# FFN modulation groups of 2, 4, 6 and 4 k-tiles in a transformer block on one Trainium2 core

## The chip, the core and the metric

One core of a Trainium2 chip runs the whole program. TensorE (PE in the views) does the matmuls and transposes, with its weight loads shown apart (PEld); VectorE (DVE), ScalarE (ACT) and GpSimd (POOL) do the elementwise work; SyncE's queue (SP) issues nearly all transfers. The metric is the time of one execution on the device in microseconds, the median of several.

## The reference

The program computes one transformer block for 256 tokens of width 2048 in float32. The part that matters here is the second half, the feed-forward network with its adaptive modulation:

```python
mod = jax.nn.silu(c) @ w_ada[l] + b_ada[l]
shift_m, scale_m, gate_m, shift_f, scale_f, gate_f = jnp.split(mod, 6, axis=-1)
...
o = jnp.concatenate([o_n, o_m], axis=-1) @ w_o[l]
x = x + gate_m[:, None, :] * rms_norm(o, post_norm_mix[l])
h = modulate(rms_norm(x, pre_norm_ffn[l]), shift_f, scale_f)
f = jnp.square(jax.nn.relu(h @ w_up[l])) @ w_down[l]
x = x + gate_f[:, None, :] * rms_norm(f, post_norm_ffn[l])
```

`modulate` is `h * (1 + scale) + shift`. `w_up` is 2048 x 8192, so the contraction of the up-projection has 16 k-tiles of 128 rows. The modulation vector of each of these k-tiles needs its own 2 x 128 columns (shift and scale) of `w_ada`, over all 2048 rows.

## The kernel before

**Stages.** In order of time: input modulation and input projections, compressed and windowed attention, the second attention (`moba`) beside the first half of the output projection (`wo`), the second half of `wo`, `after_mixer`, the up-projection (`up`), the down-projection (`dps`, `dn`), the end.

**Matmuls in three products.** Weights arrive as float32 and are split in two parts: `split` (lines 539 to 545) casts a 128 x 1024 tile to fp32r on ScalarE (`hi`, L544) and subtracts it on VectorE (`lo`, L545). Each product is then three matmuls of 512 columns (`products`, lines 549 to 551): hi x hi, hi x lo and lo x hi. The split tiles have WBUFS = 5 buffers of either kind; a "spare" split goes to the pool `acc` (16 buffers) instead, which holds the 16 results `facc` of the up-projection too, and `oacc` and `xm`.

**Units and the stream.** The work of these stages is a list of units. A unit may have a load (a transfer into one of RAWBUFS = 5 raw buffers of 1 MB), a prep (the splits, or steps of a gemv) and a main (the matmuls). `Stream.run` emits loads as far ahead as raw buffers allow, preps up to AHEAD = 4 units ahead while the splits they hold stay within 5, and mains in order. The framework's scheduler then orders each engine's queue by this priority and by what is ready; `tc.high_priority()` moves work forward. Queues run in that fixed order on the chip.

**The up-projection** runs in four passes, one for each group of k-tiles in `F_GROUPS`. A pass goes over 8 blocks of 1024 output columns; a block has one unit per k-tile, and a load for each two of them. A unit makes 12 matmuls: 2 token tiles, 2 column halves, 3 products. Its sums are in PSUM banks of the pool `mm`, which has 5. At a block's end `up_done` evicts four banks: ScalarE copies them to `facc` in the first pass (L1160), VectorE adds them to `facc` in the others (L1162). The first eight units of the first pass are "token major": their main does token tile 0 of all eight and then token tile 1.

**The modulation groups.** Each group of `F_MODS` is a `mod_units`: a gemv over the 2048 rows of `w_ada`, 16 k-tiles of rows, on VectorE. The first step multiplies by a scalar (L318), the 15 others multiply and add into one tile in a chain (L323); a step's width is 256 columns per k-tile of the group. `krows` steps share a raw buffer: 4 for a group of 2 k-tiles, 2 for 4, 1 for 6. After the last step TensorE transposes the result (L377), VectorE sums it (L379), ScalarE modulates the k-tiles (L414) and casts them (L417), and VectorE subtracts (L418).

The first group's gemv runs beside `wo`, and `after_mixer` applies its modulation to the first k-tiles of each token tile as it transposes them (`x2t`, L1108); the other k-tiles are copied to `xnf` (L1115). Group i's gemv, for i of 1 to 3, is spread by `spread` over pass i - 1, from position `start` to position `at` of its units, and its last unit stands ahead of the remaining ones.

Of the kernel before, what the change touches and what calls it, by code (L numbers as in the profile page):

```python
# [48 lines left out]
M_PLAIN = 2  # L49

M_DIRECT = (3, 7, 11)
F_MODS = (4, 4, 4, 4)
F_GROUPS = ((0, 4), (4, 8), (8, 12), (12, 16))

F_FIRST = 1
F_AT = (0, 1, 2)
# [81 lines left out]
def spread(base, extra, first, last):  # L138

    out = list(base[:first])  # L140
    n = len(extra)
    at = [first + (i * (last - first)) // max(n, 1) for i in range(n)]
    i = 0
    for j in range(first, len(base) + 1):
        while i < n and at[i] <= j:
            out.extend(extra[i])
            i += 1
        if j < len(base):
            out.append(base[j])
    while i < n:  # L150
        out.extend(extra[i])
        i += 1
    return out
# [3 lines left out]
def tile_adaln_block(ctx: ExitStack, tc: tile.TileContext, x, c, w_ada, b_ada, g_pm, g_qm, w_in,  # L157
# [262 lines left out]
    def gate_units(tag, gpost, hold, whole=True):  # L420

        name = f"gate{tag}"
        acc = Acc(True)
        base = 2 * D if tag == "m" else 5 * D

        def first():
            acc.t = gp.tile([P, D], F32, tag="ga", name=name)
            nc.gpsimd.memset(acc.t, 0.0)
            nc.sync.dma_start(acc.t[0:1, :], b_ada[:, base:base + D])

        units = gemv_units(name, base, D, False, 1, acc, first)

        st = {}

        def load():
            st["raw"] = rawtile(f"{name}post")
            nc.sync.dma_start(st["raw"], gpost.partition_broadcast(P))

        def part(q):
            b = bank(f"{name}b{q}")  # L440
            qs = slice(q * 512, (q + 1) * 512)
            hi, lo = (pair(f"{name}{n}{q}", F32R).rearrange("p a b -> p (a b)") for n in ("hi", "lo"))
            split2(acc.t[:, qs], hi, lo)
            nc.tensor.matmul(b, onesr, hi, start=True, stop=False)
            nc.tensor.matmul(b, onesr, lo, start=False, stop=True)
            nc.vector.tensor_mul(acc.t[:, qs], b, st["raw"][:, qs])
            hold["G"] = acc.t

        def main():
            for q in range(4):  # L450
                part(q)

        hold["part"] = part
        if whole:
            units.append(Unit(load, None, main, free="main"))
        else:
            units.append(Unit(load))
        return [[u] for u in units]
# [59 lines left out]
    def token_major(us, between=None, parts=1):  # L518


        halves = [u.half for u in us]

        def main():
            for t in range(NT):
                if t and parts > 1:
                    for n in range(parts):
                        for h in halves:
                            h(t, (n,))
                else:
                    for h in halves:  # L530
                        h(t)
                if between is not None:
                    between(t)

        for u in us[:-1]:
            u.main, u.rel = None, 0
        us[-1].main, us[-1].rel = main, sum(u.w for u in us)
# [15 lines left out]
    def banks(name):  # L553
        ps = {}

        def of(ci, t, first):
            if first:
                ps[ci, t] = mbank(f"{name}_{ci}_{t}")
            return ps[ci, t]

        return of
# [411 lines left out]
    def call(f):  # L973
        return [Unit(None, None, f)]

    def in_units(name, k0, k1):

        c0, parts, dsts = blocks[name]
        return weight_units(f"in_{name}{k0}", w_in, list(range(k0, k1)), c0, parts, hs,
                            banks(f"in_{name}{k0}"), in_done(name, dsts, parts), plain=M_PLAIN)  # L980

    def flat(lists):
        return [u for b in lists for u in b]
# [15 lines left out]
    base = flat(in_units(n, 0, 2) for n in ("kv", "kw", "qn", "vm", "km")) + turn0[:2]  # L999
    stream.add(spread(base, mods[1], 1, len(base) - 1))  # L1000
    base = turn0[2:] + flat(in_units(n, 2, 6) for n in ("km", "vm", "qn", "kw")) + turn1[:4]
    base.insert(3, Unit(None, late_constants))
    stream.add(spread(base, mods[2], 0, len(base) - 3))
    base = turn1[4:] + flat(in_units(n, 6, 10) for n in ("kw", "qn", "vm", "km")) + turn2[:4]
    stream.add(spread(base, mods[3], 0, len(base) - 3))
    base = turn2[4:]
# [3 lines left out]
    base = per[0] + per[1] + call(cmp_inputs) + call(keys)  # L1010
# [45 lines left out]
    xnf, fstat = [], {}  # L1056
    k0s = np.cumsum((0,) + F_MODS).tolist()
    ffn_mods = [mod_units("f", k0, n, xnf, fstat) for k0, n in zip(k0s, F_MODS)]

# [6 lines left out]
    def keep_mod(k0, n, last):  # L1066
        def main():
            f = last.reduce()
            x2h["mod"].update((k, f(k)) for k in range(k0, k0 + n))
        return [Unit(None, None, main)]  # L1070

    first_mods = [g for k0, n, m in zip(k0s, F_MODS, ffn_mods[:F_FIRST])
                  for g in m[:-1] + [keep_mod(k0, n, m[-1][0])]]
# [6 lines left out]
    def after_mixer(t):  # L1080

        x2 = x2h["x"]
        n0 = F_GROUPS[0][1]
        if t == 0:
# [68 lines left out]
    def up_done(blk, g):  # L1153
        def done(ci, t, b):
            n = blk * 2 + ci
            if n not in facc:
                facc[n] = chunk(f"facc{n}")
            dst = facc[n][:, t, :]
            if g == 0:
                nc.scalar.copy(dst, b)  # L1160
            else:
                nc.vector.tensor_add(dst, b, dst)  # L1162
            if g == len(F_GROUPS) - 1:
                nc.scalar.activation(dst, dst, AF.Relu)  # L1164
                if t == NT - 1:
                    later.append(n)
        return done
# [5 lines left out]
    gf = gate_units("f", g_qf, gate_f, False)  # L1173
    for g, span in enumerate(F_GROUPS):
        ks = list(range(*span))
        lastg = g == len(F_GROUPS) - 1
        base = []
        for blk in range(NB):
            name = f"up{g}_{blk}"
            spare = ((1,), (1, 3))[blk] if g == 0 and blk < 2 else ()  # L1180
            us = weight_units(name, w_up, ks, blk * 1024, C2, fs, banks(name), up_done(blk, g),
                              spare)
            if lastg and blk:
                us = us[:2] + call(later_unit) + us[2:4] + call(later_unit) + us[4:]
            base += us
        extra = [u for i, m in enumerate(ffn_mods) for u in m
                 if i >= F_FIRST and g == F_AT[i - F_FIRST]]
        if g == 0:
            token_major(base[:8])
        start = 8 if g == 0 else 2  # L1190
        at = len(base) - 6
        stream.add(spread(base[:at], extra[:-1], start, at) + flat(extra[-1:])
                   + base[at:])

# [128 lines left out]
```

## Time and profile before

| | |
|---|---|
| median of 3 runs | 1191.05 us (1190.25 to 1193.13) |
| the profiled execution: its time | 1188.98 us |
| its span | 1187.2 us |
| TensorE busy | 1154.3 us, 97% |
| VectorE busy | 901.4 us, 76% |
| ScalarE busy | 592.8 us, 50% |
| read from HBM | 308.99 MB |
| first pass of the up-projection begins | 457.27 us |
| VectorE's first addition of the second pass begins | 560.41 us |

The span is what the profiler's records cover; the execution's own time is a little longer. Busy is the time in which an engine has at least one instruction in work. Matmuls overlap: one shows 0.39 us and the next starts 0.23 us after it, so a busy TensorE may still have gaps that the view doesn't show. The granted clock is a share of 2.4 GHz.

### The profile page before, as it was taken

How to read it: one execution, taken by the hardware profiler on the slowest of the kernel's cores; microseconds unless marked ns; L12 is line 12 of the kernel's file. 1: busy time of each engine (PE TensorE's matmuls, PEld its weight loads, DVE VectorE, ACT ScalarE, POOL GpSimd, SP SyncE). 2: the span in 40 equal slices, each digit the busy share in tenths (PEclk: the TensorE clock that was granted, in tenths of full speed). 3: DMA queues.
4: the chain of work that ended last, by engine and by line, in shares of the span. 5: the costliest groups of instructions: out<-in, count | busy, mean ns of one | idle time of the engine just before them, and what ended most of it. 6: DMA issues, size and time to landing. Idle time of an engine off the chain costs nothing.

```text
span 1187.2 us, 14413 instructions
## 1 busy us (share of the span) xinstructions
PE 1154.3 (97%) x5411; PEld 935.7 (79%) x5411; DVE 901.4 (76%) x1111; ACT 592.8 (50%) x908; POOL 13.5 (1%) x23
## 2 busy tenths in 40 slices
PE   5999999999999998999999999999999999999997
PEld 4468888877777786888888888888888888888885
DVE  5679999889999988777888986666576666665573
ACT  4353444438746658565343344767444434444441
POOL 1000000000000001000000000000000000000000
PEclk9999999999999999999999999999999999999999
DMA  9999998775867985988878976545677777775541
GB/s 333 370 394 326 334 362 295 238 281 176 316 213 258 327 337 200 367 285 305 290 249 300 315 248 204 172 152 208 238 244 270 255 258 264 259 268 187 203 142 71
DMA packets 92601, 312.03 MB, mean 263 GB/s; under 512 B 6306, under 2 KB 14962, under 8 KB 79602
## 3 DMA queue, kind: packets, MB, share of 16 engines
q1 hardware_dynamic: 92324, 311.04, 74.7%
q8 instruction: 42, 0.69, 0.2%
q14 instruction: 27, 0.22, 0.1%
q10 hardware_dynamic: 208, 0.07, 0.0%
HBM read 308.99 MB, written 2.10 MB: 262 GB/s over the span
## 4 chain that ended last, share of the span: by engine, by line
PE 88%; DVE 7%; ACT 1%; issue 1%; DMA 1%; POOL 0%; SPq 0%; DVEq 0%; POOLq 0%; ACTq 0%
PE dps L550 10%; PE dps L551 10%; PE dps L549 10%; PE up L551 9%; PE up L550 9%; PE up L549 9%; PE wo L550 2%; PE wo L549 1%; PE wo L551 1%; PE ft L1146 1%; PE in_qm L551 1%; PE in_qm L549 1%; PE in_qm L550 1%; PE in_km L549 1%; PE in_km L550 1%
## 5 line engine op out<-in xcount | busy, mean ns | idle before, releaser
L323 DVE SCALAR_TENSOR_TENSOR modm<-modm,csil,modm 128x1024 f32<-128x1024 f32 (+1 forms) x72 | 78.3, 1087 | 9.4 <-DMA modm<-in_w_ada_dram 8.0
L323 DVE SCALAR_TENSOR_TENSOR modf<-modf,csil,modf 128x1024 f32<-128x1024 f32 x60 | 76.8, 1280 | 5.6 <-DMA modf<-in_w_ada_dram 5.2
L1162 DVE TENSOR_TENSOR facc<-up,facc 128x512 f32<-128x512 f32 x96 | 61.5, 685 | 19.2 <-PE up L551 19.2
L323 DVE SCALAR_TENSOR_TENSOR gatef<-gatef,csil,gatef 128x1024 f32<-128x1024 f32 x32 | 40.6, 1280 | 1.7 <-DMA gatef<-in_w_ada_dram 1.7
L323 DVE SCALAR_TENSOR_TENSOR gatem<-gatem,csil,gatem 128x1024 f32<-128x1024 f32 x32 | 40.3, 1275 | 0.0
L1202 DVE TENSOR_TENSOR flo<-facc,fhi 128x512 fp32r<-128x512 f32 x32 | 21.8, 686 | 2.0 <-ACT fhi L1201 2.0
L1201 ACT CAST fhi<-facc 128x512 fp32r<-128x512 f32 x32 | 19.7, 624 | 5.3 <-PE up L550 1.9
L1164 ACT ACTIVATE facc<-facc 128x512 f32<-128x512 f32 x32 | 18.4, 623 | 2.8 <-DVE facc L1162 2.8
L1160 ACT COPY facc<-up 128x512 f32<-128x512 f32 x32 | 18.0, 586 | 1.7 <-PE up L551 1.0
L545 DVE TENSOR_TENSOR up_13lo<-up,up_13hi 128x1024 fp32r<-128x1024 f32 x8 | 9.8, 1226 | 11.5 <-ACT up_13hi L544 11.5
L545 DVE TENSOR_TENSOR up_14lo<-up,up_14hi 128x1024 fp32r<-128x1024 f32 x8 | 9.8, 1226 | 11.1 <-ACT up_14hi L544 11.1
L1151 ACT ACTIVATE facc<-ft 128x512 f32<-128x512 f32 x32 | 17.1, 586 | 0.4 <-PE ft L1146 0.2
L1146 PE MATMUL ft<-ident,facc 128*128 128x128 f32 x128 | 16.8, 273 | 0.0
L1146 PEld LDWEIGHTS ft<-ident,facc 128*128 128x128 f32 x128 | 14.7, 140 | 2.6 <-ACT facc L1151 0.4
L544 ACT CAST up_7hi<-up 128x1024 fp32r<-128x1024 f32 x8 | 8.4, 1056 | 14.2 <-PE up L551 14.2
L544 ACT CAST up_11hi<-up 128x1024 fp32r<-128x1024 f32 x8 | 8.4, 1056 | 14.2 <-PE up L551 14.2
L544 ACT CAST up_10hi<-up 128x1024 fp32r<-128x1024 f32 x8 | 8.4, 1056 | 13.3 <-PE up L551 13.3
L544 ACT CAST up_6hi<-up 128x1024 fp32r<-128x1024 f32 x8 | 8.4, 1056 | 13.3 <-PE up L551 13.3
L544 ACT CAST up_14hi<-up 128x1024 fp32r<-128x1024 f32 x8 | 8.4, 1049 | 12.6 <-PE up L551 12.6
L544 ACT CAST up_9hi<-up 128x1024 fp32r<-128x1024 f32 x8 | 8.4, 1056 | 12.1 <-DVE up_8lo L545 6.7
L544 ACT CAST up_8hi<-up 128x1024 fp32r<-128x1024 f32 x8 | 8.4, 1054 | 11.7 <-PE up L551 11.7
L544 ACT CAST up_5hi<-up 128x1024 fp32r<-128x1024 f32 x8 | 8.4, 1056 | 11.2 <-PE up L551 7.8
(2266 smaller groups left out, 3966.4 us busy)
## 6 DMA issues: line engine op xcount, KB each, us to landing
up<-in_w_up_dram SPq DMA_DIRECT2D x64, 1024.0 KB, 5.2
dn<-in_w_down_dram SPq DMA_DIRECT2D x64, 1024.0 KB, 5.0
modf<-in_w_ada_dram SPq DMA_DIRECT2D x64, 512.0 KB, 6.2
modm<-in_w_ada_dram SPq DMA_DIRECT2D x48, 512.0 KB, 7.1
gatem<-in_w_ada_dram SPq DMA_DIRECT2D x16, 1024.0 KB, 5.5
wo<-in_w_o_dram SPq DMA_DIRECT2D x16, 1024.0 KB, 6.3
gatef<-in_w_ada_dram SPq DMA_DIRECT2D x16, 1024.0 KB, 4.9
modm<-in_w_ada_dram SPq DMA_DIRECT2D x32, 256.0 KB, 6.0
```

The costliest lines, as they stand in the source:

```text
L323: nc.vector.scalar_tensor_tensor(part, w[:, j:j + step], csil[:, k:k + 1], part, ALU.mult, ALU.add)
L544: nc.scalar.copy(hi[:, 0:n], src)
L545: nc.vector.tensor_sub(lo[:, 0:n], src, hi[:, 0:n].bitcast(F32))
L549: nc.tensor.matmul(o, shi, whi, start=first, stop=False)
L550: nc.tensor.matmul(o, shi, wlo, start=False, stop=False)
L551: nc.tensor.matmul(o, slo, whi, start=False, stop=last)
L1146: nc.tensor.transpose(b[:, (2 * i + t) * P:(2 * i + t + 1) * P], f[:, t, (2 * j + i) * P:(2 * j + i + 1) * P], ident)
L1160: nc.scalar.copy(dst, b)
L1162: nc.vector.tensor_add(dst, b, dst)
L1164: nc.scalar.activation(dst, dst, AF.Relu)
L1201: nc.scalar.copy(hi, f)
L1202: nc.vector.tensor_sub(lo, f, hi.bitcast(F32))
```

## The change

The groups become 2, 4, 6 and 4 k-tiles, and the passes cover the same k-tiles as the groups. The number of passes, matmuls, weight loads and evictions stays. In the first pass each block now has two units instead of four, so the eight token-major units are four blocks and not two; the three spare splits go to the second k-tile of the first three blocks. The gemv of the second group is spread over positions 6 to 13 of the first pass's 16 units.

```diff
-F_MODS = (4, 4, 4, 4)
-F_GROUPS = ((0, 4), (4, 8), (8, 12), (12, 16))
+F_MODS = (2, 4, 6, 4)
+F_GROUPS = ((0, 2), (2, 6), (6, 12), (12, 16))
...
-            spare = ((1,), (1, 3))[blk] if g == 0 and blk < 2 else ()
+            spare = (1,) if g == 0 and blk < 3 else ()
...
-        start = 8 if g == 0 else 2
-        at = len(base) - 6
+        start = 6 if g == 0 else 2
+        at = len(base) - (3 if g == 0 else 6)
```

## Rows read from the trace of the kernel before

**Rows 1.** The page, busy time, share of the span and instructions of TensorE.

```profile
PE 1154.3 (97%) x5411; PEld 935.7 (79%) x5411; DVE 901.4 (76%) x1111; ACT 592.8 (50%) x908; POOL 13.5 (1%) x23
```

**Rows 2.** What TensorE waited for, whole span: total, times, longest.

```profile
PE wo L550 <- DVE wo_10lo L545: 1.6, 1, 1.6
PE x2t L1108 <- issue: 1.6, 2, 1.2
...
PE up L549 <- ACT xmhi L417: 1.1, 1, 1.1
...
PE up L550 <- DVE up_2lo L545: 1.0, 1, 1.0
```

**Rows 3.** Busy time by stretch, then granted clock, DMA share, GB/s.

```profile
384.00:400.00 16.00, 16.00 (x78) 13.02 (x78) 15.96 (x25) 8.65 (x22) 0.00 (x0) 1.00 0.83 273
400.00:418.00 18.00, 16.33 (x83) 12.97 (x82) 17.40 (x21) 11.75 (x23) 0.00 (x0) 1.00 1.01 366
420.00:430.00 10.00, 10.00 (x46) 8.29 (x45) 9.72 (x11) 6.32 (x7) 0.00 (x0) 1.00 1.02 411
457.30:484.00 26.70, 24.24 (x113) 19.50 (x112) 24.44 (x33) 21.55 (x48) 2.45 (x2) 1.00 0.93 328
469.20:484.00 14.80, 13.34 (x66) 10.79 (x65) 13.27 (x14) 11.94 (x24) 0.11 (x1) 1.00 0.99 342
484.00:506.00 22.00, 22.00 (x98) 18.22 (x98) 16.36 (x15) 11.89 (x16) 0.00 (x0) 1.00 0.99 365
548.00:635.60 87.60, 87.60 (x392) 72.59 (x391) 75.89 (x82) 38.69 (x42) 0.00 (x0) 1.00 0.80 282
```

**Rows 4.** TensorE in order of time, two block starts of the first pass.

```profile
457.27 0.39 PE L549 MATMUL up<-up_0hi,xmhi 128*128 128x512 f32 x1
...
462.71 0.39 PE L549 MATMUL up<-up_0hi,xmhi 128*128 128x512 f32 x1
```

**Rows 5.** VectorE's groups by shape: whole span, and the first from 457.3 to 506.

```profile
L323 DVE SCALAR_TENSOR_TENSOR modf<-modf,csil,modf 128x1024 f32<-128x1024 f32 x12 | 15.4, 1281 | 1.3 <-DMA modf<-in_w_ada_dram 1.3
...
L323 DVE SCALAR_TENSOR_TENSOR modf<-modf,csil,modf 128x1024 f32<-128x1024 f32 x60 | 76.8, 1280 | 5.6 <-DMA modf<-in_w_ada_dram 5.2
...
L323 DVE SCALAR_TENSOR_TENSOR modm<-modm,csil,modm 128x512 f32<-128x512 f32 x27 | 20.6, 761 | 0.7
...
L379 DVE TENSOR_REDUCE modf8red<-modf8t 128x4 f32<-128x512 f32 x2 | 1.3, 682 | 0.0
```

**Rows 6.** VectorE in order of time, beside the output projection and in pass two.

```profile
410.68 3.92 DVE L323 SCALAR_TENSOR_TENSOR modf<-modf,csil,modf 128x1024 f32<-128x1024 f32 x3
414.52 1.22 DVE L545 TENSOR_TENSOR wo_10lo<-wo,wo_10hi 128x1024 fp32r<-128x1024 f32 x1
...
565.08 1.28 DVE L323 SCALAR_TENSOR_TENSOR modf<-modf,csil,modf 128x1024 f32<-128x1024 f32 x1
566.27 1.22 DVE L545 TENSOR_TENSOR up_5lo<-up,up_5hi 128x1024 fp32r<-128x1024 f32 x1
...
570.41 0.69 DVE L1162 TENSOR_TENSOR facc<-up,facc 128x512 f32<-128x512 f32 x1 [0.58 <-PE up L551]
```

**Rows 7.** ScalarE in order of time at the second token half.

```profile
465.88 0.63 ACT L1096 ACTIVATE xa<-x 128x512 f32<-128x512 f32 x1
...
466.51 1.05 ACT L1160 COPY facc<-up 128x512 f32<-128x512 f32 x2
...
471.06 1.15 ACT L414 ACTIVATE xm<-x2t,modf0red 128x128 f32<-128x128 f32 x3
472.10 0.41 ACT L417 CAST xmhi<-xm 128x256 fp32r<-128x256 f32 x1
```

**Rows 8.** SyncE's queue in order of time, issues around the first pass's start.

```profile
428.53 26.16 SPq L476 DMA_DIRECT2D up<-in_w_up_dram  x4
456.13 0.88 SPq L305 DMA_DIRECT2D modf<-in_w_ada_dram  x2
```

**Rows 9.** The transfers of `modf`, 512 KB each: issue to landing.

```profile
DMA to landing us min/median/max: 3.5/6.2/9.6
```

## The prediction

> **What bounds the kernel now.** I read the page first. TensorE is busy for 97% of the span [rows 1], so a change that leaves the matmuls as they are can win only what TensorE waits, and can lose whatever new wait it makes. The second view is the list of TensorE's waits [rows 2]: between 380 and 484 us, the stretch that the change touches, the rows are 1.6 us for the last output-projection weights (`wo_10lo`, VectorE late), 1.6 us before the transposes of the normalized x, 1.1 us for the first modulated tile of the second token half (`xmhi`), and 1.0 us for `up_2lo`. From 484 us to the end of the up-projection there is practically no wait. So at most some 5 us are to be had, and not all by this change.
>
> The third view is the table of stretches [rows 3]. It shows what lies right behind TensorE. In 384 to 400 us VectorE is busy for 15.96 of 16 us and TensorE loses nothing; in 400 to 418 us VectorE has 17.40 of 18 and TensorE loses 1.67. There the gemv of the first modulation group runs beside the output projection. In the first pass of the up-projection the DMA share is 0.93 to 0.99; in the second pass (548 to 635.6) VectorE is busy for 75.89 of 87.6 us. The granted clock is 1.00 throughout (the 2.4 GHz level), in spite of the short gaps, so gaps of 1 or 2 us cost only themselves. Where VectorE or the transfers are squeezed further, TensorE is next to feel it.
>
> **The change part by part.**
>
> *TensorE's own work* does not change. A pass over n k-tiles has n x 8 blocks x 2 token tiles x 2 column halves x 3 products, 96n matmuls of 512 columns; 24 of them took 5.44 us (457.27 to 462.71, [rows 4]), 0.227 each. The passes so become 43.5, 87.0, 130.6 and 87.0 us in place of four of 87.0: the same sum. The transposes of the gemv results are 4, 8, 12 and 8, 32 as before. Also 128 evictions remain: 32 copies in pass one, 96 additions in the others.
>
> *The gemv work is resized.* 16 rows of 512, 1024, 1536 and 1024 columns: the same elements and the same bytes in all. A 1024-wide step takes 1280 ns, a 512-wide one 761 [rows 5], so 512 columns are worth 0.52 us, and I estimate a 1536-wide step at 1.80 us. Where such steps are mixed with others, they start 1.19 us apart (565.08 to 566.27, [rows 6]), so a 1536-wide one would hold VectorE for about 1.71.
>
> *Before the up-projection* the first group's gemv falls by 16 x 0.52 = 8.3 us of VectorE and by 4.2 MB of transfers. This is where `wo_10lo` was late: three gemv steps (410.68, 3.92 us) ran ahead of it [rows 6]. With half of that work gone I count the whole wait as won: **-1.6 us** (bounds -1.6 and 0; nothing else waits in that stretch that this could shorten).
>
> *The entry into the up-projection.* The head of each token half now modulates 2 k-tiles instead of 4. The first `xmhi` came after three modulations that ended near 472.1 [rows 7]; with two of them it comes 0.4 us earlier. Against that, the token-major head is now four blocks of two k-tiles, not two blocks of four. Its first half fills 8 PSUM banks of a pool of 5, where it filled 4, and the third block's second bank is wanted after 27 matmuls, at 457.27 + 6.1 = 463.4, when ScalarE's first two eviction copies ran only at 466.51 [rows 7], because the squares of the second token half hold ScalarE. If that order stays, TensorE stands 3.7 us there. But its second half cannot start before `xmhi` anyway: the first half (48 matmuls, 10.9 us) would be through at 468.2, the transposes of x take 2.1, and `xmhi` is ready about 472.5, so 2.2 us of the stall are covered, and 1.5 remain. The weights of the fourth block lead to the same place: before, all four loads of the head were issued between 428.53 and 454.69, ahead of any gemv load (456.13, [rows 8]); now two 1 MB gemv loads stand ahead of the fourth in the queue. Bounds -0.4 and +2.2; nearer to the stall row than to nothing, since both effects meet the same cover, I take **+0.6 us**.
>
> *The first pass* shrinks to 43.5 us and must now hide a whole 4-tile gemv (16 steps, 8.4 MB). VectorE: from 457.3 to 506 it was busy 24.44 + 16.36 = 40.8 us [rows 3], with 12 of the group's 15 chained steps in it [rows 5]. By the new end of the pass (457.3 + 43.5 + 2.1 + 0.9 of transposes + 2.5 of waits and 0.6 from the entry, about 507) it must have done the other 3 steps too (3.6), the sums (two of 0.68, [rows 5], and small ones, 1.5) and a first split (0.6), less one split of 0.4: 46 of 50 us, 92%. Transfers: the weights of the seventh block stand behind 8 gemv loads and three weight loads, the 12th MB after 456.13. At the 365 GB/s of 484 to 506 us [rows 3] that is 12 x 2.87 = 34.5 us, and 2 us for landing (the shortest gemv piece took 3.5 us, of which 1.4 is its transfer, [rows 9]): 492.7. At the 328 GB/s of 457 to 484 it is 496.6. Then come the cast and the subtraction, 2.3 us. TensorE wants these weights four units of 2.72 us after the head, at about 495.5. So the pass is 0.5 us early at the one rate and 3.4 late at the other.
>
> *The second pass* keeps its 87.0 us but now hides a 6-tile gemv. VectorE had 75.89 us of work there, about as much of the next group's gemv done ahead as its own had been. To it come 15 x 0.52 + 0.3 for the wider steps and about 1.2 for one more sum and one more split: 85.2 of 88.3 us, 97%. The gemv loads are spread over 24 of the 32 units, so nearly all of the excess lies in the first 65 us.
>
> *The third pass* has 130.6 us for a 4-tile gemv and gains air, but TensorE waits for nothing there before, so that gives nothing back. Pass four is as before.
>
> *What the squeeze costs.* No row shows such a pass, so I go by the nearest: 34 us (384 to 418) with VectorE at 98% and the transfers at 0.83 to 1.01 cost TensorE 1.67 us. The first pass after its head (some 23 us) and the gemv part of the second (65 us) are 88 us of that kind: 88 x 1.67 / 34 = **+4.3 us**. The bounds are 0 (384 to 400 alone lost nothing) and 88 x 1.67 / 18 = 8.2 (all of it as in 400 to 418).
>
> **Sum:** -1.6 + 0.6 + 4.3 = +3.3 us. The profiled execution took 1188.98 us in all, span 1187.2, so 1192.3 on that scale; it ran 2.07 us below the median of the runs shown, 1191.05, and against the median I predict **1194.3 us**. What a measurement can tell from no change is about 0.3%, 3.6 us: the forecast lies just inside it.
>
> **The rivals.**
>
> *A, the passes hide it all.* VectorE at 99.75% with no loss (384 to 400) speaks for it; the DMA share of 0.99 in the first pass speaks against. Then -1.6 and -0.4 remain: 1189.0 us; if the 1.6 before the transposes goes as well, because VectorE and the queue run ahead, 1187.4. Chance 0.25, of which 0.11 for more than 3.6 us won.
>
> *B, evictions get stuck in pass two.* At a block's end TensorE wants the first block's bank back 12 matmuls, 2.72 us, after it finished with it. An addition (0.69, [rows 6]) behind a 1536-wide step and a split (1.80 + 1.22) would end 3.7 us after, 1.0 late, for two banks of each of 8 blocks. This decides once both stand ahead of the addition in VectorE's order. With the 1280-ns step the same queue ends at 3.2 and no wait was seen, which speaks against it. Price up to 8 us in place of the 4.3 of the sum, with the first pass's share of 1.1 kept: 1199 us. Chance 0.13.
>
> *C, the transfers bind.* At 328 GB/s pass one is 3.4 us late; in pass two, 24 units bring 24 MB, 25.2e6 bytes, which take 69 us at 365 GB/s and 73.6 at the 342 of 469 to 484 us [rows 3], against 65.4 of TensorE: some 4 to 8 us, less a lead of 5 buffers. With both about +7 in place of 4.3, and the entry at its +2.2: 1199 us. Against it speaks that the trace moved 411 GB/s in 420 to 430 us [rows 3]: at that rate the 24 MB take 61.3. The Trainium skill (DMA: Bandwidth & Descriptors, Specifications) gives about 358 GB/s as the HBM limit of a core. The row is above it, so it is no ceiling in this trace; by the page the 24 MB would take 70.3 us, an estimate, and C would be likelier than I make it. Chance 0.10.
>
> *Forecast* (partial stalls, -1 to +7 on the sum): 0.52, split 0.30 within 0.3% and 0.22 above.
>
> **The numbers.** Faster 0.11; same 0.14 + 0.30 = 0.44; slower 0.22 + 0.13 + 0.10 = 0.45. The range takes A's first case and B and C in and leaves out about 2 in 10: 1188.0 to 1200.0. The forecast's own range is 1190 to 1198.
>
> **What the profile after would show.** The wait for `wo_10lo` is gone. TensorE stands 1 to 4 us between 460 and 475 at a bank or the fourth block's weights. The gemv of k-tiles 2 to 5 ends within 10 us of the first pass's end, and waits for `up_..lo` sum to 1 to 3 us before it and 2 to 5 us in the second pass, where VectorE is busy for over 93%. If the waits there sum to under 1 us, the squeeze term is wrong and A holds; if TensorE waits for additions (`facc`), B holds; if VectorE waits long for `modf` loads, C.

## The result and the profile after

The changed kernel took 1199.53 us in the median (1197.63 to 1201.16, 6 runs) against 1190.65 us (6 runs of the kernel before beside it): a ratio of 1.0074, 95% interval 1.0058 to 1.0089, or 8.9 us more. The forecast of 1194.3 us had the direction; the time lies 0.5 us inside the upper end of the range, which reached that far only for the rivals B and C (1199 us each), and more than twice the forecast amount was lost.

TensorE's waits after, for the whole span (total, times, longest), answer to [rows 2]:

```profile
PE x2t L1108 <- issue: 4.5, 2, 3.3
...
PE up L550 <- DVE up_2lo L545: 1.6, 2, 1.3
PE up L549 <- ACT facc L1160: 1.3, 1, 1.3
...
PE up L549 <- DVE facc L1162: 1.0, 2, 0.7
...
PE up L550 <- DVE up_0lo L545: 0.8, 1, 0.8
PE up L550 <- DVE up_1lo L545: 0.8, 1, 0.8
```

The wait for `wo_10lo` is gone, as forecast. In its place stand a long one before the transposes of x, one for an eviction copy, and many small ones for split weights of the up-projection. The list names the engine that released TensorE last; it doesn't say what held that engine. The stretches after, with columns as in [rows 3]:

```profile
418.00:455.00 37.00, 35.80 (x167) 29.53 (x166) 25.59 (x37) 21.04 (x44) 1.10 (x2) 1.00 0.42 150
455.00:480.00 25.00, 20.39 (x91) 16.70 (x90) 21.07 (x28) 18.55 (x41) 2.63 (x2) 0.93 0.99 357
480.00:500.00 20.00, 19.14 (x88) 15.38 (x87) 16.37 (x17) 13.23 (x21) 0.00 (x0) 1.00 0.99 372
510.00:530.00 20.00, 20.00 (x90) 16.55 (x89) 19.44 (x18) 8.83 (x10) 0.00 (x0) 1.00 0.99 367
530.00:550.00 20.00, 20.00 (x88) 16.18 (x87) 17.58 (x17) 6.08 (x6) 0.00 (x0) 1.00 0.88 309
550.00:570.00 20.00, 18.48 (x78) 13.95 (x76) 18.84 (x19) 5.99 (x6) 0.00 (x0) 1.00 0.88 319
570.00:590.00 20.00, 18.69 (x89) 15.28 (x88) 19.42 (x24) 11.81 (x17) 0.00 (x0) 1.00 0.99 363
...
509.20:575.00 65.80, 64.28 (x279) 51.46 (x278) 61.62 (x56) 22.79 (x25) 0.00 (x0) 1.00 0.92 333
```

The stretches from 455 to 500 and from 510 to 530 us have a DMA share of 0.99, at 357 to 372 GB/s, right after 37 us at a share of 0.42; from 530 to 570 the share is 0.88, at 309 to 319. Over the part of the second pass that carries gemv loads (last row) it is 0.92, at 333 GB/s. What TensorE loses lies mostly after 455 us. Note the matmul counts: 78 in 550 to 570, against the 88 or 90 that go into 20 us; counts show more than the busy time does.

For the sum, I counted the matmuls of the up-projection in order of time and took the time from the first of each stage to the first of the next. The head is the eight token-major units. 96 matmuls take 21.8 us and each transpose 0.11, so that without waits the rest of the first pass would take 22.7 us in the changed kernel and its second pass 88.4.

```
                 up starts  head  rest of 1st   2nd    3rd    4th, to the down-projection
before (4,4,4,4)   457.27   26.8     66.4      87.9   88.0     99.6
after  (2,4,6,4)   452.85   30.6     25.7      93.0  132.4    100.0
```

The up-projection starts 4.4 us earlier. Of that, 1.6 are no part of the change: the first `wo` matmul, ahead of anything it touches, already stands at 325.1 in place of 326.7 us. The head takes 3.8 us more, and the four passes behind it 351.1 in place of 341.9, or 9.2 more; 3.0 of these are waits of the first pass, 4.6 of the second, about 0.9 of the third. Together -4.4 + 3.8 + 9.2 = +8.6 us, the difference of the spans (1195.8 and 1187.2).

### The profile page after: what moved, and what is told of

Same layout as the page of the kernel before. It is cut to its first block, busy times and chain, and to the rows that moved or that the text cites. A ratio compares the mean times of both kernels' runs of the same rounds, so it can differ in the third digit from the quotient of the medians.

```text
span 1195.8 us, 14418 instructions
## 1 busy us (share of the span) xinstructions
PE 1156.1 (97%) x5411; PEld 933.9 (78%) x5411; DVE 901.8 (75%) x1110; ACT 591.3 (49%) x907; POOL 13.7 (1%) x23
## 4 chain that ended last, share of the span: by engine, by line
PE 85%; DVE 8%; issue 2%; DMA 2%; ACT 2%; POOL 0%; SPq 0%; DVEq 0%; POOLq 0%; ACTq 0%
PE dps L549 10%; PE dps L551 10%; PE dps L550 10%; PE up L550 9%; PE up L551 9%; PE up L549 9%; PE wo L549 2%; PE wo L551 2%; PE wo L550 2%; PE ft L1146 1%; PE in_qm L551 1%; PE in_qm L550 1%; PE in_qm L549 1%; DVE modm L323 1%; PE in_km L550 1%
## 5 line engine op out<-in xcount | busy, mean ns | idle before, releaser
L323 DVE SCALAR_TENSOR_TENSOR modf<-modf,csil,modf 128x1024 f32<-128x1024 f32 (+2 forms) x60 | 76.7, 1279 | 2.9 <-DMA modf<-in_w_ada_dram 2.6
L544 ACT CAST up_4hi<-up 128x1024 fp32r<-128x1024 f32 x8 | 8.4, 1052 | 22.6 <-DMA up<-in_w_up_dram 20.6
L544 ACT CAST up_2hi<-up 128x1024 fp32r<-128x1024 f32 x8 | 8.4, 1054 | 21.8 <-DMA up<-in_w_up_dram 17.6
L545 DVE TENSOR_TENSOR up_7lo<-up,up_7hi 128x1024 fp32r<-128x1024 f32 x8 | 9.8, 1225 | 9.6 <-ACT up_7hi L544 9.6
L544 ACT CAST up_8hi<-up 128x1024 fp32r<-128x1024 f32 x8 | 8.4, 1055 | 12.6 <-PE up L551 12.6
L544 ACT CAST up_14hi<-up 128x1024 fp32r<-128x1024 f32 x8 | 8.4, 1050 | 12.6 <-PE up L551 12.6
L550 PE MATMUL up<-up_2lo,modf2hi 128*128 128x512 f32 x32 | 13.0, 405 | 1.6 <-DVE up_2lo L545 1.6
```

The source lines that it names most:

```text
L323: nc.vector.scalar_tensor_tensor(part, w[:, j:j + step], csil[:, k:k + 1], part, ALU.mult, ALU.add)
L544: nc.scalar.copy(hi[:, 0:n], src)
L545: nc.vector.tensor_sub(lo[:, 0:n], src, hi[:, 0:n].bitcast(F32))
L550: nc.tensor.matmul(o, shi, wlo, start=False, stop=False)
```

## The experiments

All ratios are to runs of the kernel before on the same chip. The table of their stages stands at the end of this section.

**1. The second group's gemv starts later (`r1_start8`).** The theory after the result was that its loads came too early in the queue.

```diff
-        start = 6 if g == 0 else 2
+        start = 8 if g == 0 else 2
```

> The changed kernel with the second group's gemv spread from position 8 instead of 6, so that the fourth block's weights stand ahead of all its loads in the queue. Between the first matmul of the up-projection and the end of its eight token-major units the changed kernel took 30.6 us, the one before 26.8. Theory Q (the two gemv loads ahead of the fourth block, and gemv steps in VectorE's order between the normalization's instructions, make the 3.3 us idle time before the transposes): that stretch falls to 27 to 28.5 us, the idle time under 1 us, the granted clock stays 1.00 there, and the whole is 2 to 3.5 us shorter than the changed kernel. Rival K (the eviction copies and the five PSUM banks make it): the stretch stays above 30 us and the time within 1 us of the changed kernel.

Measured: 1195.99 us, ratio 1.0047 (1.0030 to 1.0064). The head fell from 30.6 to 27.3 us. Theory Q holds for it, with 1.1 us of idle time where under 1 was laid down. The stretch in the changed kernel, VectorE and TensorE in order of time:

```profile
457.83 2.74 DVE L1094 SCALAR_TENSOR_TENSOR x<-oacc,or,xa 128x512 f32<-128x512 f32 x4 [0.44 <-POOL or L274]
...
461.62 1.28 DVE L323 SCALAR_TENSOR_TENSOR modf<-modf,csil,modf 128x1024 f32<-128x1024 f32 x1
462.82 0.15 DVE L269 TENSOR_REDUCE x2r<-x2ss 128x1 f32<-128x4 f32 x1
462.94 1.29 DVE L323 SCALAR_TENSOR_TENSOR modf<-modf,csil,modf 128x1024 f32<-128x1024 f32 x1
464.14 0.15 DVE L273 TENSOR_SCALAR x2r<-x2r 128x1 f32<-128x1 f32 x1
...
465.98 0.88 DVE L1104 TENSOR_SCALAR xa<-x,x2r 128x512 f32<-128x512 f32 x2 [0.44 <-POOL x2r L274]
...
461.18 0.50 PE L549 MATMUL up<-up_0hi,xmhi 128*128 128x512 f32 x1 [1.33 <-ACT facc L1160]
...
466.57 2.79 PE L1108 MATMUL x2t<-ident,xa 128*128 128x128 f32 x12 [3.27 <-issue]
```

Two instructions of 0.15 us in the normalization (L269, L273) each wait behind a gemv step of 1.28 us that has nothing to do with them, so that from L1094 to L1104 it is 8.2 us; the same two points were 6.2 us apart in the kernel before. Meanwhile the fourth block's weights are late: four gemv transfers stand ahead of them in SyncE's queue, and ScalarE's cast of them (467.22) stands behind L1102, which waits for the normalization:

```profile
452.69 1.91 SPq L305 DMA_DIRECT2D modf<-in_w_ada_dram  x4
455.36 0.37 SPq L476 DMA_DIRECT2D up<-in_w_up_dram  x1
```

So TensorE has neither the rest of the first token half nor the second. Its idle time has a sequel in the granted clock (last columns: clock, DMA share, GB/s):

```profile
463.00:466.50 3.50, 0.30 (x2) 0.00 (x0) 3.06 (x5) 1.69 (x4) 1.58 (x1) 0.96 0.95 310
466.50:470.00 3.50, 3.43 (x16) 3.27 (x17) 3.23 (x5) 3.50 (x10) 0.00 (x0) 0.55 1.02 376
```

After 3.3 us without a matmul the clock is 0.55 over the next 3.5 us, so mostly at its lower level of 1.2 GHz, and the twelve transposes take 2.79 us. In the experiment the weights go first, the idle time is 1.1 us, the clock stays 1.00, and they take 1.50:

```profile
454.53 0.37 SPq L476 DMA_DIRECT2D up<-in_w_up_dram  x1
455.56 2.52 SPq L305 DMA_DIRECT2D modf<-in_w_ada_dram  x4
```

```profile
467.84 1.50 PE L1108 MATMUL x2t<-ident,xa 128*128 128x128 f32 x12 [1.11 <-issue]
```

The wait for the eviction copy is gone as well; ScalarE's first copies now run at 458.4. The passes stayed slow: 26.9 us for the rest of the first, 92.4 for the second.

**2. The wide gemv alone (`r2_wide`).** The kernel before, with its third group's gemv made 6 k-tiles wide:

```diff
+        WL = 6 * P if tag == "f" and k0 == 8 else W
...
-        units = gemv_units(name, base + k0 * P, W, True, min(1024 // W, 4), acc, first,
+        units = gemv_units(name, base + k0 * P, WL, True, min(1024 // WL, 4), acc, first,
```

> The kernel before with one thing added: the gemv of its third group (k-tiles 8 to 11, hidden by the second pass) is made 6 k-tiles wide in transfers and steps, and only the 4 it needs are used; the passes stay 4, 4, 4, 4. The second pass of the changed kernel took 4.7 us more than its matmuls and transposes, that of the kernel before about nothing. Theory S (a 6-tile gemv is more than a pass of 87 us hides, by itself): the second pass takes 3 to 6 us more than its matmuls and transposes, and the time rises by 3 to 6 us over the kernel before. Rival L (the second pass loses only because the short first pass leaves it late, with buffers empty): under 1.5 us there and in the time.

Measured: 1190.99 us, ratio 0.9997 (0.9986 to 1.0009). The second pass took 87.9 us, as before. Theory S falls: a 6-tile gemv is not in itself more than a pass of 87 us hides.

**3 and 4. Without the steps, without the transfers (`r3_nosteps`, `r4_noloads`).** Both are the changed kernel, with the second and third group changed:

```diff
+                    if name in ("modf2", "modf6"):
+                        n = step = 8
                     for j in range(0, n, step):
```

> The changed kernel without most of VectorE's gemv work in the second and third group: all transfers stay, but each multiply-add covers 8 columns instead of 1024 or 1536, so the modulation of these k-tiles is not the reference's. That takes some 17 us of VectorE out of the first pass and 25 out of the second. Theory V (VectorE is what binds in the two passes): the first pass after its head and the second pass lose under 1 us each in place of 2.9 and 4.7, and the time is 6 to 8 us below the changed kernel. Rival D (the transfers bind): the first pass still loses 2 us or more and the second 3 or more, and the time falls by 2 us at most.

```diff
+                    w = acc.t[:, 0:n] if i and name in ("modf2", "modf6") else st["raw"][:, kk * n:(kk + 1) * n]
...
+            if i and name in ("modf2", "modf6"):
+                units.append(Unit(None, prep, None))
```

> The changed kernel without the transfers of the second and third group's gemv after the first raw buffer's: the steps keep their width and read their own accumulator in place of the weights, so the modulation of these k-tiles is not the reference's. That takes 7.3 MB out of the first pass and 11.8 MB out of the second, and the raw buffers with them. Theory D (the transfers bind): the first pass after its head and the second lose under 1 us each, and the time falls by 6 us or more. Rival V (VectorE binds): the losses stay at 2 us or more and 3 us or more, and the time falls by 3 us at most, which would be the entry's, since no gemv load stands ahead of the fourth block's weights any more.

Measured: 1198.28 us without the steps, ratio 1.0058 (1.0042 to 1.0075), and 1189.47 without the transfers, 0.9991 (0.9979 to 1.0003). Without the steps the rest of the first pass still took 27.6 us; the second pass fell to 90.2. Theory V falls with that, and Rival D holds but for the second pass, which lost 1.8 us in place of 3 or more. Without the transfers they took 22.8 and 88.4: no wait is left, as Theory D said. VectorE's whole work remained, and the stretches show how little that matters:

```profile
484.90:507.60 22.70, 22.70 (x105) 18.74 (x104) 22.62 (x23) 18.00 (x30) 0.00 (x0) 1.00 0.67 228
507.60:596.00 88.40, 88.40 (x397) 73.34 (x396) 85.65 (x88) 40.10 (x45) 0.00 (x0) 1.00 0.59 203
```

VectorE is busy for 22.62 of 22.70 and 85.65 of 88.40 us, and TensorE never waits.

The run without the steps tells something of the head, too. There L1094 and L1104 stand 5.0 us apart in place of 8.2, and still the head took 31.4 us, because TensorE then waited for the cast of the fourth block's weights, which ScalarE did only at 469.43:

```profile
470.60 0.73 PE L551 MATMUL up<-up_0hi,xmhi 128*128 128x512 f32 x2 [2.24 <-ACT up_0hi L546]
```

So taking the steps away doesn't mend the head by itself; this speaks for the earlier weights as what experiment 1 gains by.

**5. Half the bytes (`r5_half`).** The run before took away the bytes and the raw buffers together. This one keeps buffers, units and step widths:

```diff
+                if name == "modf6":
+                    nc.sync.dma_start(v[:, 0, 0], src[:, 0, 0])
+                    return
-                for kk in range(krows):
+                for kk in range(1 if name == "modf2" else krows):
                     nc.sync.dma_start(v[:, kk], src[:, kk])
```

> The changed kernel with half the bytes in the gemv transfers of its second and third group: the same raw buffers, units and step widths, but two steps (second group) or the two halves of a step (third group) read the same loaded part, so the modulation of these k-tiles is not the reference's. Taking the transfers and their raw buffers away altogether brought the first pass after its head from 25.7 to 22.8 us and the second pass from 93.0 to 88.4. Theory R (the rate of the DMA engines binds): with half the bytes the two are back at 22.8 to 23.5 and 88.3 to 89.5, and the time is 6 us or more below the changed kernel. Rival N (the five raw buffers and the order of the queue bind, not the bytes): the first pass after its head stays above 24.5 and the second above 91, and the time falls by 3 us at most.

Measured: 1189.70 us, ratio 0.9999 (0.9989 to 1.0010); 23.8 us for the rest of the first pass (up to 23.5 had been laid down), of which 0.6 is a wait for the last gemv step, and 88.4 for the second. Its second pass:

```profile
506.00:594.00 88.00, 88.00 (x396) 72.98 (x395) 86.18 (x89) 38.79 (x43) 0.00 (x0) 1.00 0.82 283
```

In the second pass it is the bytes that cost, and Rival N falls. That the DMA engines' own rate is the limit, as Theory R has it, is more than the run shows: the second pass of the changed kernel moved 333 GB/s at a share of 0.92, where the same kernel moved 372 in 480 to 500 us. A load can be issued only when one of the five raw buffers is free again (between 509 and 602 us the up-projection's loads waited ten times, 24.5 us in all, for a gemv step to end), so with fewer bytes the buffers also fill sooner. VectorE at 98% with TensorE at 100% says once more that it is not VectorE alone. What ScalarE's casts of the up-projection's weights waited for from 508 to 600 us (total, times, longest) shows it directly, first in the changed kernel, then with half the bytes:

```profile
ACT up_4hi L544 <- DMA up<-in_w_up_dram: 20.6, 5, 7.1
ACT up_2hi L544 <- DMA up<-in_w_up_dram: 17.6, 4, 6.3
```

```profile
ACT up_5hi L558 <- PE up L565: 13.0, 7, 3.0
...
ACT up_2hi L558 <- DMA up<-in_w_up_dram: 3.4, 1, 3.4
```

With all the bytes the casts wait for transfers, 38 us in all, and TensorE runs out of split weights; with half of them they wait for TensorE to give buffers back, as they should. In the first pass it is not so plain. There, in the changed kernel, ScalarE waits for no transfer at all, but for TensorE:

```profile
492.51 1.95 ACT L1160 COPY facc<-up 128x512 f32<-128x512 f32 x3 [2.81 <-PE up L551]
494.36 1.05 ACT L544 CAST up_0hi<-up 128x1024 fp32r<-128x1024 f32 x1
...
497.51 1.59 ACT L414 ACTIVATE xnf<-xnf,modf2red 128x256 f32<-128x256 f32 x3 [0.67 <-DVE modf2red L384]
...
500.02 1.03 ACT L544 CAST up_0hi<-up 128x1024 fp32r<-128x1024 f32 x1
```

An engine's queue has an order that is fixed when the kernel is built. In it the cast for the seventh block (494.36) stands behind the copies of the block before, which wait for TensorE, and that of the eighth (500.02) behind the modulation. With half the bytes the build put both casts ahead of those, at 488.66 and 491.77. So the two runs differ in order too, and the first pass needed a run of its own (experiment 10).

**6 and 7. Less asked of the second pass (`r6_2446`, `r7_spread`).** Both have experiment 1's edit; one moves the 6-tile gemv to the third pass, the other spreads it over 27 units:

```diff
-F_MODS = (2, 4, 6, 4)
-F_GROUPS = ((0, 2), (2, 6), (6, 12), (12, 16))
+F_MODS = (2, 4, 4, 6)
+F_GROUPS = ((0, 2), (2, 6), (6, 10), (10, 16))
```

> The changed kernel with the second group's gemv from position 8, as in the run before, and groups and passes of 2, 4, 4 and 6, so that the second pass hides a 4-tile gemv and the third, of 87 us, the 6-tile one. Theory P (the second pass loses because weights and gemv together ask for more than the DMA rate of 365 GB/s over its first 24 units, 25.2 MB in 65 us, and it starts without a lead): it now asks for 21.0 MB, and loses under 1.5 us in place of 4.1; the third pass starts with a lead and loses under 1.5; the time is 1191 to 1193. Rival E (what was lost is the lead, and a pass that starts without one loses whatever its gemv): the second pass still loses 3 us or more, and the time stays near 1196.

```diff
-        at = len(base) - (3 if g == 0 else 6)
+        at = len(base) - (6 if g == 2 else 3)
```

> The changed kernel with the second group's gemv from position 8 and the third group's gemv spread over 27 units of the second pass in place of 24. Theory P (the asked rate over the units that carry gemv): the asked rate falls from 385 to some 365 GB/s, and the second pass loses 2 to 3 us in place of 4.1. Rival E (the lead): no change within 1 us in that pass, or a loss at the third pass's start because the gemv ends too late.

Measured: 1191.70 us, ratio 1.0014 (1.0005 to 1.0023), for the groups of 2, 4, 4 and 6; 1193.57, ratio 1.0024 (1.0013 to 1.0036), for the wider spread. In the first the second pass took 87.9 us, no wait at all, though it followed the same late first pass (26.9 us); the third, which hides 6 tiles in 87 us, took 89.2, 0.8 more than its work. In the other the second pass took 89.6, 1.2 more than its work in place of 4.0. Rival E falls: a pass without a lead loses nothing if it asks for less than the rate. Theory P's forecasts hold, a little better than its numbers; its 365 GB/s as the rate that binds is not shown (the 27 units brought 345, where the 24 had brought 333).

**8. Later gemv in the kernel before (`r8_wolate`).** Is the good part to be had alone?

```diff
-    o1 = (spread(o1[:-8], extra[17:], 0, len(o1) - 12)
+    o1 = (spread(o1[:-8], extra[17:], 0, len(o1) - 8)
```

> The kernel before with one edit: the last gemv units of its first group are spread over 8 units of the output projection in place of 4. It asks whether the part of the change that helped (the wait for the split of the output projection's weights, 1.6 us) can be had without the shorter first pass. If the crowding of gemv steps made that wait: the wait is gone and the time 1 to 2 us below the kernel before, at the edge of what can be told. If VectorE's total work in that stretch made it: the wait moves to a later weight tile and the time stays.

Measured: 1192.87 us, ratio 1.0025 (1.0017 to 1.0034). The wait for `wo_10lo` did go, but a larger one came: the twelve transposes of the first token half waited 4.41 us, and the up-projection started at 462.41.

```profile
458.91 2.79 PE L1108 MATMUL x2t<-ident,xa 128*128 128x128 f32 x12 [4.41 <-issue]
```

VectorE did the last five splits of `wo` only from 435.7 to 441.5 us, and the normalization's instructions stood between splits behind them. Neither outcome that was laid down came; the wait moved, and grew.

**9. Five groups (`r9_22444`).** If the rate asked in the first pass is the matter, a smaller second group should cure it. The gemv starts from position 8 here, too.

```diff
-F_MODS = (2, 4, 6, 4)
+F_MODS = (2, 2, 4, 4, 4)
...
-F_AT = (0, 1, 2)
+F_AT = (0, 1, 2, 3)
...
-        at = len(base) - (3 if g == 0 else 6)
+        at = len(base) - (3 if g < 2 else 6)
```

> The changed kernel with five groups and passes of 2, 2, 4, 4 and 4 k-tiles, the second group's gemv from position 8, and the gemv of the first two passes spread up to 3 units before their end. There are 32 more evictions, as additions on VectorE. Theory P (a pass loses when the weights and the gemv spread over its units ask for more than some 365 GB/s and no lead is left): the first pass hides only a 2-tile gemv, 4.2 MB in place of 8.4, and its rest after the head falls to 22.3 to 23 us; the second, of 43.5 us, hides a 4-tile gemv, asks for 386 GB/s with a full lead from the first pass, and loses under 2 us; the others lose nothing. With the 2 to 3 us won before the up-projection that gives 1188 to 1191, at or just under the kernel before. Rival X (each short pass loses as the changed kernel's first one did, through evictions or late splits, whatever the rate): the second pass loses 3 us or more, and the time is 1193 or more.

Measured: 1195.26 us, ratio 1.0038 (1.0025 to 1.0051). The first pass did as Theory P said: 22.4 us for its rest, no wait (what part the order had in that, see experiment 10). The second took 52.9 in place of 44.4, where I had left VectorE out of the sum:

```profile
525.00:550.00 25.00, 19.78 (x85) 14.43 (x84) 25.00 (x32) 10.67 (x14) 0.00 (x0) 1.00 0.78 268
```

```profile
PE up L549 <- DVE facc L1162: 3.5, 4, 1.6
PE up L550 <- DVE up_3lo L545: 1.9, 2, 1.1
```

A pass of two k-tiles that adds its sums has 32 additions (0.6 us from one to the next), 16 splits (1.14) and 15 gemv steps of 1.2 on VectorE: 55 us and more in 44.4. There VectorE does bind, 25.00 of 25.00 us, at a DMA share of 0.78. Theory P missed the second pass and the time. Rival X is right about both, and the waits are those it named, additions (the evictions of this pass) and late splits; it is wrong about the first pass, which lost nothing.

**10. Another order in the first pass (`r10_first`).** Experiment 1's kernel, with the splits of the last two blocks built ahead:

```diff
+                    if name in ("up0_6", "up0_7"):
+                        with tc.high_priority():
+                            st[kk] = split(st["raw"][:, kk * ncol:(kk + 1) * ncol],
+                                           f"{name}_{ks[i0] + kk}", i0 + kk in spare)
+                        return
                     hi, lo = split(st["raw"][:, kk * ncol:(kk + 1) * ncol], f"{name}_{ks[i0] + kk}",
```

> Experiment 1's kernel, in which the splits of the first pass's seventh and eighth block are built with a higher priority, so that their casts stand ahead of most of the modulation's instructions on ScalarE (xnf, L414, and modf2hi, L417), and their subtractions ahead of modf2lo (L418) on VectorE; the seventh block's first split stays behind the four eviction copies of the block before and behind the sums of the gemv (modf2red). No transfer is touched. Theory O (the waits of the first pass are made by the fixed order on ScalarE and VectorE, the weights have landed by then): the new places bring the casts of the eighth block from 500 to before 498 without a wait for a DMA, and the rest of the first pass falls from 26.7 to 25 to 26 us; the second pass stays at 92 to 93 us; 1194 to 1196 us. Theory D (the weights themselves come too late): ScalarE then waits for the transfer of up at these casts, between 492 and 500 us, and the rest of the first pass stays at 26.5 to 27 us.

Measured: 1195.0 us, ratio 1.0045 (1.0032 to 1.0059), which can't be told from experiment 1's 1.0047; the profile can. The rest of the first pass fell from 26.9 us (the 26.7 of the expectation is a miscount) to 25.6, and the eighth block's casts ran without any wait for a transfer, a little later than laid down (498.75):

```profile
498.75 1.03 ACT L549 CAST up_0hi<-up 128x1024 fp32r<-128x1024 f32 x1
```

Theory O holds for the eighth block: the weights lay there. What is left of the wait is VectorE's order, five gemv steps in a row and then the sums, ahead of the seventh block's split, while TensorE waits 0.91 and 1.56 us:

```profile
488.16 6.56 DVE L323 SCALAR_TENSOR_TENSOR modf<-modf,csil,modf 128x1024 f32<-128x1024 f32 x5
...
497.14 1.22 DVE L550 TENSOR_TENSOR up_0lo<-up,up_0hi 128x1024 fp32r<-128x1024 f32 x1
```

The second pass took 92.5 us as before, so the 1.3 us won at the end of the first brought it nothing.

The stages of all runs, as in the table above (us):

```
                            up starts  head  rest of 1st   2nd    3rd
after             (2,4,6,4)   452.85   30.6     25.7      93.0  132.4
1 gemv from 8     (2,4,6,4)   454.70   27.3     26.9      92.4  132.0
2 wide gemv       (4,4,4,4)   459.47   26.8     66.5      87.9   88.0
3 no steps        (2,4,6,4)   455.35   31.4     27.6      90.2  132.3
4 no transfers    (2,4,6,4)   456.29   28.6     22.8      88.4  131.9
5 half the bytes  (2,4,6,4)   453.46   28.5     23.8      88.4  132.3
6                 (2,4,4,6)   453.95   27.3     26.9      87.9   89.2
7 wider spread    (2,4,6,4)   455.26   27.3     26.9      89.6  132.1
8 later gemv      (4,4,4,4)   462.41   25.2     66.4      88.9   88.0
9              (2,2,4,4,4)   454.23   26.0     22.4      52.9   87.9
10 order          (2,4,6,4)   455.66   27.3     25.6      92.5  131.7
```

The starts differ by some 2 us without any edit's doing: experiment 2 changes nothing ahead of the up-projection and starts at 459.47, the kernel before at 457.27.

No version beat the kernel before; the nearest that does the whole computation, experiment 6, is 0.14% slower.

## Why the prediction was right or wrong

**Before the up-projection: right, and more.** The forecast was the whole wait of 1.6 us. In the changed kernel 96 `wo` matmuls in a row (the 205th to the 300th) took 21.8 us, their pure time, in place of 24.9; besides the wait, eight transposes of the gemv had stood among them before, and the four that are left now stand elsewhere.

**The entry: the mechanism was named, the cover was wrong.** The step reckoned that what the bank and the fourth block's weights cost beyond 2.2 us would be paid, since the second half could not start before 472.5 us anyway; +0.6, at most +2.2. The head lost 3.8. Its start was earlier by 4.4 us, so the second half became ready near 469.5, but two things were missing from the sum: gemv steps between the normalization's own instructions (2 us), and the lower clock after the idle time (the transposes 1.3 us longer). Experiment 1 moves the transfers and wins 3.3 us of the 3.8 back. It moves the steps as well; experiment 3, without the steps and with the transfers where they were, has a head of 31.4 us, so the steps alone are not the cause. The prediction also took it that gaps of 1 or 2 us cost only themselves, from rows whose longest is 1.6 us [rows 2]; a lower clock behind a longer one it counted nowhere.

**The first pass: the size of the late case, by another way.** The working had the seventh block's weights 0.5 us early at 365 GB/s or 3.4 late at 328, and I then put 1.1 us into the sum. 3.0 us were lost, but not because those weights landed late: they were issued at 482.4, loads of that stretch took 7.7 us in the median, so about 490, and TensorE was ready for them at 495.5. The queues of ScalarE and VectorE have their splits behind copies, gemv steps and sums that wait (experiments 5 and 10). The step counted each engine's work and never asked in which order it stands.

**The squeeze: this is the step that failed.** It went by the stretch of 384 to 418 us, with VectorE at 98%, and scaled its 1.67 us to 4.3 over both passes. The 4.3 was 7.6 (3.0 + 4.6), near the bound of 8.2, and the likeness was the wrong one: VectorE at 98 to 99.6% costs nothing where the transfers keep up (experiments 4 and 5). What costs in the second pass is the bytes asked of the transfers: 12.6 MB of gemv rows, and 12.6 MB of the up-projection's weights with them, over the 65 us of 24 units, 385 GB/s; it got 333. With 27 units the loss is 1.2 us, with a 4-tile gemv (321 GB/s) nothing. Experiment 2 asked for the same 385 GB/s and lost nothing, though it got only 350 (552.7 to 618 us); so by these figures at least 2.3 of its 25.2 MB had landed ahead. Its transfers had 87 us of a first pass to get such a lead in, which I take to be the reason. VectorE has a part only behind the transfers: without the gemv steps, which hold raw buffers while they wait and run, the second pass loses 1.8 us instead of 4.6 (experiment 3).

**The rivals.** C, the transfers, was the right one for the larger part, at a chance of 0.10 and with 1199 us as its price. I had set 411 GB/s against it, a stretch of 10 us with the output projection's own loads [rows 3]; where gemv and up-projection weights mix, the changed kernel held 390 over 20 us at best (478 to 498) and 333 over the part of the second pass that carries gemv loads. The Trainium skill gives about 358 GB/s as the HBM limit of a core (DMA: Bandwidth & Descriptors, Specifications). I had called it no ceiling, and the 390 is above it, as is the 386 of 480 to 500 us in experiment 1. B, the evictions, made 0.7 us of one wait in the second pass. A fell.

**Left open:** whether the build chose the first pass's order because of the transfers (with half the bytes it chose another) is argued, not shown, and the seventh block's split was not brought ahead by itself. The third pass takes some 0.9 us more than its work, and no run was made for it. What keeps the second pass's transfers at 333 GB/s and a share of 0.92 is not shown: more raw buffers, which would let loads be issued sooner, were not tried, and so the rate of the transfers and the turn of the five buffers are not told apart.

## What to carry to other kernels

Before moving hidden work from one stage to another, divide the bytes that each stage must bring by its length, over the units that really carry them, and add the lead that the stage before leaves; an engine at 98% may cost nothing (experiment 4) where a second pass with a DMA share of 0.92 loses 4.6 us. A stage made shorter gives its neighbours less to hide behind: the 2.8 us won before the first pass (4.4, less 1.6 that are no part of the change) were paid for by 13 us behind it (3.8 + 9.2). And cost every engine for every new stage, with the order of its queue: the one short pass that had its transfers right (experiment 9) had 55 us of VectorE's work in 44.

## What the runs showed of the hardware that I had not expected

A single idle time of 3.3 us on TensorE was followed by a granted clock of 0.55 over 3.5 us, while waits of up to 1.64 us in the kernel before left it at 1.00 [rows 3]. The wait of 4.41 us in experiment 8 was followed by a clock of 0.50 (458.7 to 462.1 us) and by transposes of 2.79 us, in place of 1.50, too. Shorter waits can do it as well: 2.24 us for the fourth block's cast in experiment 3, with little but transposes around it, came ahead of a clock of 0.50 (472.3 to 475.6 us), and 1.89 us for `wo_10lo` in experiment 2 ahead of 0.51 (416.9 to 420.3 us). So the prediction's reading, that gaps of 1 or 2 us cost only themselves, holds for the kernel before and not for these two runs.
